# Output projection by seven block products in place of eight: where its weights, its block sums and its order stand in a three-stage encoder kernel

## The chip, the core and the metric

The kernel runs on one NeuronCore of one Trainium2 chip. The core's engines each run their own instruction stream: TensorE (PE in the profile, with its weight loads as PEld), VectorE (DVE), ScalarE (ACT), GpSimd (POOL) and SyncE (SP), which here issues all DMAs. The metric is the device time of one execution in microseconds (us); less is better.

## The reference

One encoder layer over two token streams (a sample of 2048 tokens and a prompt of 1024, both of width 1024). Two branches share one input projection: neighbourhood attention (8 heads of 64) and a gated DeltaNet (4 heads of 128). The last part is what the change touches:

```python
y_a = jnp.einsum('bte,ed->btd', o_a, w_branch_a)
y_b = jnp.einsum('bte,ed->btd', o_b, w_branch_b)
merged = jax.nn.sigmoid(gate_a) * y_a + jax.nn.sigmoid(gate_b) * y_b
return x + jnp.einsum('btd,de->bte', merged, w_out)
```

`o_a` and `o_b` have 512 columns, `merged` and `w_out` have 1024. All data is float32. The kernel writes each float32 operand as a sum of two float16 parts, high and low, scaled by powers of two, and makes each matrix product of three float16 products: high by high, high by low, low by high.

## The kernel before

**Three stages.** The DeltaNet stage makes the hidden activations, the DeltaNet output and the gates, and leaves them in DRAM (`obd`, `szd`, `gtd`). The attention stage loops over four pairs of heads. For each pair it runs 24 projection tiles (`proj_mm`, 24 matmuls `ppn` each) and 24 attention units, one unit and one projection tile per `slot`. A unit runs through several slots: scores (`pS`), softmax, transposes (`pT`), values (`pon`). After the last projection tile the remaining units run in slots of their own; this is called the tail below. The attention output goes to DRAM as `oad`. The output stage takes the tokens in 12 chunks of 256, in the order of the list `order`.

**A chunk of the output stage.** `chunk` loads both branch outputs (`x`), their gate (`y` or `z`) and the sigmoid gates (`th`), multiplies one gate in on POOL (`x<-x,y`), takes the absolute maximum over the chunk (DVE `om<-x`, then a PE transpose `pm` that spreads it over the partitions, then DVE `om<-pm` and three small instructions for a power of two), and splits `x` into high and low parts `op` (ACT high, DVE low). `merged` runs, for each of 8 column tiles `e`, two groups of 12 matmuls of 256 columns (`py_`), one per branch. DVE multiplies each by its gate (`th<-th,py_`), POOL adds the two (`th<-th,th`), ACT and DVE split the sum into `mm`. The output product then runs, for two halves of 128 tokens and two halves of 512 columns, 8 x 3 matmuls of 512 columns (`po_`), and DVE adds each result to the input tile `xo`, which is stored. That is 192 matmuls of 256 columns and 96 of 512 in a chunk.

**What sets the order.** In the DeltaNet and attention stages PE, DVE and ACT are pinned: they keep the order in which the program names the instructions (`TP`, `VP`, `SP` for the attention stage). POOL and SP are ordered by a scheduler. In the output stage before the change all engines are left to the scheduler (`T`, `V`, `S`, `G`, `SY`). Each engine works through its stream in order, so an instruction that waits holds up all behind it. All these calls go through one helper, so the profile shows them all on line 61, and tiles are told apart by name. In the program text the functions stand at: `proj_mm` 1414, `block_out` 1576, `branch_weights` 1597, `early` 1627, `slot` 1653, the tail's loop 1716, `chunk` 1727, `merged` 1754, the output loop 1789.

**Weights.** `w_out` (4 MB) is loaded by 128-column strips and split into `woh` and `wol` at the start of the output stage. In the last pair of the attention stage `branch_weights` loads and splits 16 tiles of `w_branch_a` and `w_branch_b` (ACT `y<-wst,abp`, DVE `y<-wst,abp,y`).

Of the kernel before, what the change touches and what calls it, by code (L numbers as in the profile page):

```python
# [45 lines left out]
def emit(nc, tc, x_prompt, x_sample, norm_g, w_in, attn_q_norm_g, attn_k_norm_g, attn_rpb, dn_conv_w, dn_a_log,  # L46
# [1267 lines left out]
    ps_S = opn("n_S", bufs=NPS[1], space=PSUM)  # L1314
    ps_T = opn("n_T", bufs=NPS[2], space=PSUM)
    ps_O = opn("n_O", bufs=NPS[3], space=PSUM)
    p_mm, ps_mm = pool("n_mm", bufs=NPS[0], side="right", space=PSUM)
    p_Q, ps_Q = pool("n_Q", bufs=1, side="right", space=PSUM)
# [43 lines left out]
    def load_weights(n, src, hi, lo, done, s=None):  # L1362

        def load():
            st = wk.tile([128, src.shape[0] // 128, src.shape[1]], F32, name="wst", tag="xt", bufs=XB)
# [61 lines left out]

    def proj_parts(w, b, t, pp):

        qs = wk.tile([128, 384], F32, name="qs", bufs=QSB)  # L1430
        SP.activation(qs, pp, AF.Copy, scale=2.0 ** -20)
        sq = wk.tile([128, 4, 64], F32, name="sqn", bufs=SQB)
        SP.activation(sq.rearrange("p a b -> p (a b)"), qs[:, 0:256], AF.Square)
        vt = wk.tile([128, 2, 128], F16, name="vt")
# [140 lines left out]

    def block_out(u):

        pO = ps_Q.tile([128, BLK], F32, name="pO", tag="Q") if p_g is None else ps_O.tile([128, BLK], F32, name="pO", tag="o")
        for cb in range(4):
            TP.transpose(pO.rearrange("p (r c) -> p r c", c=64)[:, :, 16 * cb:16 * cb + 16], u.Os[:, cb], ident)  # L1580
        dst = lambda d: d[u.b][128 * u.w.hp:128 * u.w.hp + 128, :]
# [5 lines left out]
            SY.dma_start(dst(oad), ot)  # L1587

        at(0, "dve2", gate)

    def split(src, s, hi, lo, bufs):
        kt = src.shape[0] // 128
        st = wk.tile([128, kt, src.shape[1]], F32, name="wst", tag="xt", bufs=bufs)
        SY.dma_start(st, src.rearrange("(k p) c -> p k c", p=128))
        whl(hi, lo, st, s)

    def branch_weights(n):

# [25 lines left out]
    load_H(4)  # L1624
    load_H(5)

    def early():

        nonlocal ps_g, p_g
        for p in (p_Q, p_mm):  # L1630
            close(p)
        p_g, ps_g = pool("p_g", bufs=3, side="right", space=PSUM)

    ps_g = p_g = None

# [17 lines left out]
    def slot(mm):  # L1653
# [21 lines left out]
        if t:  # L1675
            C.append(t)
        run("dve1")
        for u in E:
            unit_exp(u)
        E.clear()  # L1680
# [8 lines left out]
            B.append((sn + 2, u))  # L1689
        run("act2")  # L1690
        run("dve2")
        work(PW[5], mm)
        sn += 1

    for hp_ in range(4):
        if hp_:
            w = nxt
        if hp_ < 3:
            nxt = pair(hp_ + 1)
            next_pair(nxt)  # L1700
        for b, ats in ((4, ()), (5, (4,)), (0, ()), (1, (0,)), (2, (1,)), (3, (2, 3, 5))):
            if hp_ == 3 and b == 0:
                branch_weights(0)
            for t in range(4):
                mm = proj_mm(w, b, t)
                slot(mm)
                work(1, mm)
# [3 lines left out]
            for a in ats:  # L1711
                for cb in range(4):
                    u = K()
                    u.w, u.b, u.cb = w, a, cb
                    units.append((sn + LA, u))
    while units or B or C or later:
        if p_g is None and done == 48:
            early()
        slot(iter(()))


    order = [8, 9, 0, 1, 2, 3, 4, 5, 6, 7, 10, 11]

    def big(name, *shape):
        return hr.tile([128, *shape], F32 if len(shape) == 3 else F16, name=name, tag="h", bufs=8)

    def chunk(i, pool, **kw):

        c = K()
        c.i, cs = i, slice(TB * (i % 2), TB * (i % 2) + TB)  # L1730
        x = big(f"x{i}", 2, 4, TB)
        y = big(f"y{i}", 2, 4, TB)
        ob, sz = x[:, 1], y[:, 0]
        for t, d in ((x[:, 0], oad), (ob, obd), (sz, szd)):
            SY.dma_start(t, d[i // 2].rearrange("(k p) t -> p k t", p=128)[:, :, cs])
        c.th = [big(f"th{i}{j}", 2, 4, TB) for j in range(2)]
        for j in range(2):
            SY.dma_start(c.th[j].rearrange("p a k t -> p (a k) t"), gtd[i].rearrange("(e j) p t -> j p e t", j=2)[j])
        G.tensor_tensor(ob, ob, sz, op=MUL)
        m = sm.tile([128, 1], F32, name="om")  # L1740
        V.tensor_reduce(m, x.rearrange("p a k t -> p (a k t)"), axis=AX.X, op=MAX, apply_absolute_value=True)
        m2 = sm.tile([128, 1], F32, name="om2")
        allmax(sm, m2, m, (ps_g, "g", 1))
        c.pp, s = sm.tile([128, 1], F32, name="opp"), sm.tile([128, 1], F32, name="osp")
        pow2(m2, c.pp, s, 14)
        op = pool.tile([128, 2, 2, 4, TB], F16, name="op", **kw)
        c.o = [(op[:, j, 0], op[:, j, 1]) for j in range(2)]
        for j in range(2):
            whl(*c.o[j], x[:, j], s)
        m_ = pool.tile([128, 2, 8, TB], F16, name="mm", **kw)  # L1750
        c.mh, c.ml = m_[:, 0], m_[:, 1]
        return c

    def merged(c):

        for e in range(8):
            us = []
            for j in range(2):
                th = c.th[j].rearrange("p a k t -> p (a k) t")[:, e]
                y = ps_g.tile([128, TB], F32, name="py_", tag="g")  # L1760
                gemm(y, wy[e, j][0], wy[e, j][1], c.o[j][0], c.o[j][1], kt=4, t1=TB)
                V.scalar_tensor_tensor(th, in0=th, scalar=1.0, in1=y, op0=ADD, op1=MUL)
                us.append(th)
            G.tensor_tensor(us[0], us[0], us[1], op=ADD)
            S.activation(c.mh[:, e, :], us[0], AF.Copy, scale=2.0 ** -26)
            V.scalar_tensor_tensor(c.ml[:, e, :], in0=us[0], scalar=2.0 ** -26, in1=c.mh[:, e, :], op0=MUL, op1=SUB)

    c0 = chunk(order[0], hr, tag="h", bufs=8)
    merged(c0)
# [6 lines left out]
    ps_o = opn("p_o", bufs=4, space=PSUM)  # L1776

    XB = 4
    woh = pw.tile([128, 8, D], F16, name="woh")
    wol = pw.tile([128, 8, D], F16, name="wol")  # L1780
    for i in range(8):
        cs = slice(128 * i, 128 * i + 128)
        split(w_out[0][:, cs], so_, woh[:, :, cs], wol[:, :, cs], XB)

    fab = pw.tile([128, 1], F32, name="fab")
    V.tensor_tensor(fab, pab, po_, op=MUL)
    V.tensor_scalar_mul(fab, fab, 2.0 ** (-1 + 26 - 42))

    for n, i in enumerate(order):
        c = c1 if n else c0  # L1790
        if n < 11:
            c1 = chunk(order[n + 1], wk)
        if n:
            merged(c)
        xs, ys, t0 = (x_sample[0], y_sample[0], TB * i) if i < 8 else (x_prompt[0], y_prompt[0], TB * (i - 8))
        fo = sm.tile([128, 1], F32, name="ofo")
        V.tensor_tensor(fo, c.pp, fab, op=MUL)
        for t in range(TB // 128):
            ts = slice(128 * t, 128 * t + 128)
            xt = wk.tile([128, D], F32, name="xo", tag="xt", bufs=XB)  # L1800
            SY.dma_start(xt, xs[t0 + 128 * t:t0 + 128 * t + 128, :])
            for n2 in range(2):
                ns = slice(512 * n2, 512 * n2 + 512)
                po = ps_o.tile([128, 512], F32, name="po_", tag="o")
# [5 lines left out]
            SY.dma_start(ys[t0 + 128 * t:t0 + 128 * t + 128, :], xt)  # L1810
    for p in (p_g, p_hr, p_h1, p_nw):
        close(p)
    while stk:
        close(stk.pop())
# [24 lines left out]
```

## Time and profile before

| | |
|---|---|
| median of 3 runs (lowest, highest) | 2895.73 us (2893.43, 2900.97) |
| the profiled execution | 2903.21 us, of which its span 2901.0 us |
| mean granted TensorE clock | 0.978 |
| busy share of the span | PE 94%, PEld 75%, DVE 59%, ACT 47%, POOL 24% |
| DeltaNet stage | to 1718.7 us |
| attention stage | first projection matmul at 1724.8, last at 2310.4; last attention matmul ends at 2393.2 |
| output stage | steady from 2452.6 to the end; first chunk's branch products lie in the attention tail |

The span runs from the first to the last instruction of one execution; all views below are of that execution. A group row names the engine, the operation, the output and input tiles, the shape, the count, and behind the bar the busy time in us and the mean in ns. A timeline row begins with the start and the duration in us and ends with the idle time before it and what ended that. A busy PE is not PE at its peak, since matmuls are pipelined: the spacing of starts says more than durations.

### The profile page before, as it was taken

Reading aid. Unit: us, or ns where it says so; the run is one execution under the profiler, and the core shown is the slowest. Engines: PE = TensorE matmul, PEld = TensorE weight load, DVE = VectorE, ACT = ScalarE, POOL = GpSimd, SP = SyncE. Lnnn points to the kernel's source line nnn. Section 1 sums busy time; section 2 is a strip of 40 time slices with the busy share of each in tenths; the row PEclk is TensorE's granted clock in tenths of the full one; section 3 lists DMA queues with packets and bytes.
Section 4 is the critical chain, followed back from the end, with each engine's and each line's share of the span. In section 5 each row is a group of like instructions: output and inputs, shape, how many; then the busy total and the mean of one; then the engine's idle time right before and its main releaser. Section 6 shows DMA issues by size and latency. Waiting matters only on the chain. (4 is left out here: it accounts for less than half of the span.)

```text
span 2901.0 us, 64328 instructions
## 1 busy us (share of the span) xinstructions
PE 2733.1 (94%) x25046; PEld 2165.8 (75%) x25046; DVE 1714.1 (59%) x4253; ACT 1358.1 (47%) x3777; POOL 704.7 (24%) x1281
## 2 busy tenths in 40 slices
PE   7889999989999999999999989999999888999999
PEld 6777888978788888888789866666666554766765
DVE  7567767577575757747575324576666675443442
ACT  4445455554445545455553434666667652111110
POOL 2232111221111221122210015454444411111211
PEclk9899999999999999999999989999999998999999
DMA  7433442344533543323434357232324458343320
GB/s 255 130 112 87 122 123 83 105 137 120 135 99 95 136 130 105 90 71 100 123 103 120 108 153 186 78 100 79 105 84 122 130 162 257 117 160 131 126 78 30
DMA packets 451743, 347.10 MB, mean 120 GB/s; under 512 B 113012, under 2 KB 414960, under 8 KB 451440
## 3 DMA queue, kind: packets, MB, share of 16 engines
q1 hardware_dynamic: 451439, 343.00, 40.2%
q8 instruction: 197, 3.23, 0.5%
q14 instruction: 107, 0.87, 0.1%
HBM read 252.04 MB, written 90.86 MB: 118 GB/s over the span
## 5 line engine op out<-in xcount | busy, mean ns | idle before, releaser
L61 PE MATMUL pp<-hh,w 128*128 128x256 f16 x6912 | 1210.9, 276 | 25.1 <-DVE thz L61 12.3
L61 PEld LDWEIGHTS <-w 128*128 128x128 f16 x10368 | 1019.8, 99 | 160.8 <-issue 20.1
L61 PE MATMUL pp<-hl,w 128*128 128x256 f16 x3456 | 953.9, 276 | 1.6 <-DMA hl<-hdr 1.2
L61 PE MATMUL ppn<-whi,rh 128*128 128x384 f16 x768 | 252.1, 328 | 6.1 <-DMA rh<-hdr 6.1
L61 PEld LDWEIGHTS <-y 128*128 128x128 f16 x2304 | 226.0, 98 | 41.6 <-issue 13.4
L61 PE MATMUL ppn<-whi,rl 128*128 128x384 f16 x768 | 252.8, 329 | 0.8 <-DMA rl<-hdr 0.8
L61 PE MATMUL ppn<-wlo,rh 128*128 128x384 f16 x768 | 252.0, 328 | 0.0
L61 PEld LDWEIGHTS <-mm 128*128 128x128 f16 x1152 | 112.8, 98 | 133.4 <-issue 0.3
L61 ACT ACTIVATE thz<-pp,wfc 128x256 f32<-128x256 f32 x288 | 123.8, 471 | 175.9 <-PE pp L61 115.4
L61 PEld LDWEIGHTS <-rh 128*128 128x128 f16 x1536 | 145.6, 98 | 77.9 <-issue 8.5
L61 POOL TENSOR_TENSOR th<-th,th 128x256 f32<-128x256 f32 x96 | 69.2, 725 | 402.6 <-DVE th L61 359.7
L61 DVE TENSOR_TENSOR pl<-pT,ph 128x384 f16<-128x384 f32 (+1 forms) x192 | 110.4, 599 | 80.4 <-ACT ph L61 79.2
L61 DVE SCALAR_TENSOR_TENSOR S<-S,egl,pk 128x128 f32<-128x128 f32 x160 | 54.9, 343 | 166.0 <-PE pk L61 139.8
L61 ACT ACTIVATE vn<-pk,nbeg 128x128 f32<-128x128 f32 x176 | 64.8, 368 | 184.6 <-PE pk L61 183.7
L61 ACT ACTIVATE mm<-th 128x256 f16<-128x256 f32 x96 | 40.0, 416 | 225.5 <-POOL th L61 225.5
L61 ACT ACTIVATE Sb<-Sb,nm,pq 128x384 f32<-128x384 f32 (+1 forms) x192 | 140.1, 734 | 1.7 <-DVE nm L61 1.7
L61 DVE CUSTOM_DVE_ANT_0 Sb<-pS,bt 128x384 f32<-128x384 f32 (+1 forms) x192 | 108.4, 597 | 51.9 <-PE pS L61 27.8
L61 POOL TENSOR_TENSOR rqk<-rqk,mhalf 128x4 f32<-128x4 f32 x48 | 51.1, 1064 | 304.0 <-DVE rqk L61 303.8
L61 ACT ACTIVATE Os<-pon,rsn 128x64 f32<-128x64 f32 x192 | 49.7, 310 | 159.7 <-PE pon L61 159.0
L61 PEld LDWEIGHTS <-rl 128*128 128x128 f16 x768 | 75.4, 98 | 61.1 <-issue 29.7
L61 DVE TENSOR_REDUCE wm<-wst 128x1 f32<-128x512 f32 (+1 forms) x111 | 82.2, 761 | 60.9 <-DMA wst<-in_w_in 47.9
L61 ACT ACTIVATE raw<-pp,wfc 128x256 f32<-128x256 f32 x144 | 63.0, 473 | 116.0 <-PE pp L61 111.4
(785 smaller groups left out, 5574.5 us busy)
## 6 DMA issues: line engine op xcount, KB each, us to landing
wst<-in_w_in SPq DMA_DIRECT2D x124, 256.0 KB
gtd<-thz SPq DMA_DIRECT2D x192, 128.0 KB
hh<-hdr SPq DMA_DIRECT2D x48, 512.0 KB
hl<-hdr SPq DMA_DIRECT2D x48, 512.0 KB
th<-gtd SPq DMA_DIRECT2D x24, 1024.0 KB
vw<-vd SPq DMA_DIRECT2D x320, 64.0 KB
IT<-gd SPq DMA_DIRECT2D x48, 256.0 KB
bt<-ud SPq DMA_DIRECT2D x192, 48.0 KB
```

The lines of the kernel that those rows point to most:

```text
L61: i = f(*a, **k)
```

## The change

**Seven products.** The output product is treated as a 2 by 2 block product: `merged` in blocks of 128 tokens by 512 inputs, `w_out` in blocks of 512 by 512. Seven products of sums of blocks (S1 to S4 of `merged`, T1 to T4 of `w_out`, and five single blocks) replace eight products of single blocks. Each is 12 matmuls of 512 columns. The sums of `merged` are made by POOL in `blocks`, four additions or subtractions of 128 x 128 for each of four column pairs `p`, behind one addition of 128 x 512 for the two branches. ACT and DVE split seven blocks in place of four (`split`: pieces of 256, 128 and 512 columns). The products are combined by DVE (`plus`, eight of 128 x 512), one ACT copy and four POOL additions (`add`).

**Weights.** The seven blocks of `w_out` are made in the first three pairs of the attention stage, 16 tiles of 128 rows, by 4 loads, 2 ACT, 2 DVE and 4 POOL instructions and 1 store each (`out_weights`), kept in DRAM as `wod` and loaded as seven tiles `wo` of 1 MB: two in the tail, five after it.

**Order.** The output stage uses the pinned engines, so PE, DVE and ACT run in program order. Chunk 0 and chunk 1 are prepared by named slots at the end of the attention stage (`begin`), chunk 0's branch products are fed into the tail's slots as `filler`, 24 matmuls per slot, and in the output stage chunk n+2 is loaded and prepared while chunk n's product runs and chunk n+1's branch products precede it. The branch products use two PSUM tiles of 512 columns in place of three of 256 columns, and DVE gates both branches by one instruction. `ne` is a new pool for staging tiles.

```diff
+    def merged(c, m):
+        for p in range(4):
+            th = c.th[p // 2][:, 2 * (p % 2):2 * (p % 2) + 2]
+            for e in range(2):
+                y = ps_g.tile([128, 2, TB], F32, name="py_", tag="g")
+                for j in range(2):
+                    ...
+                posts.append((gated, th[:, e], y))
+            posts.append((blocks, c, m, p, th[:, :, 0], th[:, :, 1]))
+    def blocks(c, m, p, u, v):
+        G.tensor_tensor(u, u, v, op=ADD)
+        l, q = (x.rearrange("p a (b t) -> p a b t", b=2) for x in (u, v))
+        G.tensor_tensor(q[:, 0, 0], l[:, 0, 1], l[:, 1, 1], op=ADD)
+        G.tensor_tensor(q[:, 1, 0], l[:, 0, 0], l[:, 0, 1], op=SUB)
+        G.tensor_tensor(q[:, 0, 1], q[:, 0, 0], l[:, 0, 0], op=SUB)
+        G.tensor_tensor(q[:, 1, 1], l[:, 1, 0], q[:, 0, 1], op=SUB)
+        splits.append((c, m, p, l, q))
+    def split(n):
+        for _ in range(n):
+            c, m, p, l, q = splits.pop(0)
+            t = m(p)
+            for d, x in ((slice(0, 2), l[:, :, 0]), (slice(2, 3), l[:, 1:2, 1]), (slice(3, 7), q)):
+                ...
+                parts(x_[:, 0], x_[:, 1], x, 2.0 ** -28)
+        def product(l, r):
+            ps = ps_o.tile([128, 512], F32, name="po_", tag="o")
+            for p in range(4):
+                (mh, ml), (wh, wl) = c.m[p], (wo[r][:, 4 * p:4 * p + 4, h] for h in range(2))
+                TP.matmul(ps, mh[:, l], wh, start=p == 0, stop=False)
+                TP.matmul(ps, mh[:, l], wl, start=False, stop=False)
+                TP.matmul(ps, ml[:, l], wh, start=False, stop=p == 3)
+            return ps
+        SP.activation(u, product(L11, R11), AF.Identity, scale=fo)
+        add(x11, u)
+        yield
+        plus(u, product(S2, T2))
+        add(x12, u)
+        yield
+        plus(u, product(S3, T3))
+        add(x22, u)
+        add(x21, u)
+        yield
+        ps = product(S1, T1)
+        plus(x12, ps)
+        plus(x22, ps)
+        yield
+        plus(x11, product(L12, R21))
+        yield
+        plus(x12, product(S4, R22))
+        SY.dma_start(ys[rows[0], :], xt[0].rearrange("p a b -> p (a b)"))
+        yield
+        plus(x21, product(L22, T4))
+        SY.dma_start(ys[rows[1], :], xt[1].rearrange("p a b -> p (a b)"))
+        yield
+    def run_merged(g):
+        for n, _ in enumerate(g, 1):
+            if n % 24 == 0:
+                old = len(splits)
+                post()
+                if n % 48 == 0:
+                    split(old)
+    run_merged(filler)
+    for n in range(12):
+        ps = iter(())
+        if n < 10:
+            cs_.append(chunk(order[n + 2]))
+            ps = cs_[-1].steps
+            next(ps)
         if n < 11:
-            c1 = chunk(order[n + 1], wk)
-        if n:
-            merged(c)
-        ...
-                for k in range(8):
-                    T.matmul(po, c.mh[:, k, ts], woh[:, k, ns], start=(k == 0), stop=False)
-                    T.matmul(po, c.mh[:, k, ts], wol[:, k, ns], start=False, stop=False)
-                    T.matmul(po, c.ml[:, k, ts], woh[:, k, ns], start=False, stop=(k == 7))
-                V.scalar_tensor_tensor(xt[:, ns], in0=po, scalar=fo, in1=xt[:, ns], op0=MUL, op1=ADD)
+            run_merged(merged(cs_[n + 1], wkm if n % 2 == 0 else nwm))
+        for k, _ in enumerate(output(cs_[n])):
+            post()
+            if k == 1:
+                split(len(splits))
+            if k in (1, 3, 4, 5):
+                next(ps, None)
```

Chunk n+2's steps run at k = 1 (the maximum `om<-x`), k = 3 (the PE transpose `pm`), k = 4 (the power of two and the high parts) and k = 5 (the low parts) of chunk n's output product.

**The order on DVE, in a chunk's output product.** `xo` is the output tile, `po` a product, `u` the running sum of products, `mm` the split parts of the next chunk's merged blocks, `th` the gated branch products, `om` the maximum of the chunk after, `op` its split parts. Before the change:

```order
L61 SCALAR_TENSOR_TENSOR mm<-th_37085,mm 128x256
L61 SCALAR_TENSOR_TENSOR xo<-po__37746,ofo,xo 128x512
L61 SCALAR_TENSOR_TENSOR xo<-po__37772,ofo,xo 128x512
L61 SCALAR_TENSOR_TENSOR xo<-po__37801,ofo,xo 128x512
L61 SCALAR_TENSOR_TENSOR xo<-po__37827,ofo,xo 128x512
L61 TENSOR_REDUCE om_37866<-pm 128x1
```

and now, from the last gated branch product of the next chunk to the spread maximum:

```order
L61 SCALAR_TENSOR_TENSOR th_36865<-th_36865,py__37477 128x512
L61 SCALAR_TENSOR_TENSOR u<-po__37538,ofo,u 128x512
L61 SCALAR_TENSOR_TENSOR mm<-th_36865,mm 128x256
L61 SCALAR_TENSOR_TENSOR mm<-th_36865,mm 128x128
L61 SCALAR_TENSOR_TENSOR mm<-th_36865,mm 128x512
L61 TENSOR_REDUCE om<-x 128x1
L61 SCALAR_TENSOR_TENSOR u<-po__37564,ofo,u 128x512
L61 SCALAR_TENSOR_TENSOR xo<-po__37580,ofo,xo 128x512 x2
L61 SCALAR_TENSOR_TENSOR xo<-po__37597,ofo,xo 128x512
L61 TENSOR_REDUCE om_37561<-pm 128x1
```

The maximum over the chunk after next now stands behind the split of the next chunk's last column pair and behind the second product's sum, all in one output product.

**The order on PE, around the spread of that maximum.** `po` is an output product, `pm` the transpose that spreads the maximum, `py` a branch product with weights `y`. Before the change it stands between the last output product and the next chunk's branch products:

```order
L61 LDWEIGHTS mm
L61 MATMUL po__37827<-woh,mm 128x512
L61 MATMUL pm<-ident,om 128x128
L61 LDWEIGHTS y_31067
L61 MATMUL py__37881<-op,y_31067 128x256
```

and now between the fourth and the fifth of the seven output products:

```order
L61 LDWEIGHTS mm
L61 MATMUL po__38368<-wo_34489,mm 128x512
L61 MATMUL pm<-ident,om 128x128
L61 LDWEIGHTS mm
L61 MATMUL po__38385<-wo_34491,mm 128x512
```

The transpose has moved from the end of the chunk's product to three products before its end.

More of the change, by code (lines that the diff above doesn't have):

```diff
@@ L1576, in block_out @@
     def block_out(u):
[L1578 removed]
+        pO = ps_Q.tile([128, BLK], F32, name="pO", tag="Q")
         for cb in range(4):
@@ new lines, in early, with load_block, out_weights, load @@
+    def early():
+        nonlocal ws, p_ws
+        close(p_ne)
+        p_ws, ws = pool("ws", side="right")
+        for r in (R11, T2):
+            load_block(r, ws)
+    def load_block(r, pool):
+        wo[r] = pool.tile([128, 16, 2, 128], F16, name=f"wo{r}")
+        SY.dma_start(wo[r], wod[r])
+    def out_weights(n, i):
+        p, q = divmod(i, 4)
+        def load():
+            st = ne.tile([128, 4, 128], F32, name="wst", tag="xt", bufs=XB)
+            with tc.issue_after(anchors["last"].ins):
+                for j, (k, c) in enumerate(((0, 1), (0, 0), (1, 0), (1, 1))):
+                    SY.dma_start(st[:, j], w_out[0][256 * p + 128 * k:256 * p + 128 * k + 128, 512 * c + 128 * q:512 * c + 128 * q + 128])
+            at(1, "act", high, st)
+        def high(st):
+            t = ne.tile([128, 7, 2, 128], F16, name="wos", tag="xt", bufs=XB)
+            SP.activation(t[:, 0:3, 0], st[:, 1:4], AF.Identity, scale=so4)
+            at(0, "dve2", low, st, t)
+        def low(st, t):
+            VP.scalar_tensor_tensor(t[:, 0:3, 1], in0=st[:, 1:4], scalar=so4, in1=t[:, 0:3, 0], op0=MUL, op1=SUB)
+            G.tensor_tensor(st[:, 0], st[:, 0], st[:, 1], op=SUB)
+            G.tensor_tensor(st[:, 3], st[:, 3], st[:, 0], op=SUB)
+            G.tensor_tensor(st[:, 2], st[:, 2], st[:, 3], op=SUB)
+            G.tensor_tensor(st[:, 1], st[:, 3], st[:, 1], op=SUB)
+            at(1, "act", sums, st, t)
+        def sums(st, t):
+            SP.activation(t[:, 3:7, 0], st, AF.Identity, scale=so4)
+            at(0, "dve2", rest, st, t)
+        def rest(st, t):
+            VP.scalar_tensor_tensor(t[:, 3:7, 1], in0=st, scalar=so4, in1=t[:, 3:7, 0], op0=MUL, op1=SUB)
+            SY.dma_start(wod[:, :, i].rearrange("r p h c -> p r (h c)"), t.rearrange("p r h c -> p r (h c)"))
+        at(n, "dma", load)
@@ L1638, in emit @@
+    ws = p_ws = None
+    wod = dr.tile([7, 128, 16, 2, 128], F16, name="wod")
+    wo = {}
+    so4 = pcn.tile([128, 1], F32, name="so4")
+    V.tensor_scalar_mul(so4, so_, 0.25)
     units, B, C, E, sn, done = [], [], [], [], 0, 0
@@ L1691, in slot, with begin, load @@
         run("dve2")
+        old = len(splits)
+        post()
+        split(old)
         work(PW[5], mm)
         sn += 1
+    cs_ = []
+    nwm = lambda p: nw.tile([128, 2, 7, 128], F16, name="mm", tag=("whi", "wlo")[p % 2], bufs=2)
+    wkm = lambda p: wk.tile([128, 2, 7, 128], F16, name="mm", bufs=4)
+    def begin(i, ns):
+        cs_.append(chunk(i))
+        def load():
+            with tc.issue_after(anchors["last"].ins):
+                next(cs_[-1].steps)
+        for n, e, f in zip(ns, ("dma", "dve2", "pe", "dve2", "dve2"), (load, *[next] * 4)):
+            at(n, e, f, *() if f is load else (cs_[-1].steps,))
     for hp_ in range(4):
@@ L1700, in emit @@
             next_pair(nxt)
+            for i in range(6 if hp_ < 2 else 4):
+                out_weights(16 + 2 * i, 6 * hp_ + i)
         for b, ats in ((4, ()), (5, (4,)), (0, ()), (1, (0,)), (2, (1,)), (3, (2, 3, 5))):
@@ L1704, in emit @@
             for t in range(4):
+                if hp_ == 3 and b == 3 and t == 2:
+                    begin(order[0], (0, 3, 4, 4, 5))
                 mm = proj_mm(w, b, t)
@@ L1715, in emit @@
                     units.append((sn + LA, u))
+    close(p_mm)
+    p_g, ps_g = pool("p_g", bufs=2, side="right", space=PSUM)
+    filler = iter(())
+    n = 0
+    PW = PT
     while units or B or C or later:
-        if p_g is None and done == 48:
+        if ws is None and done == 48:
             early()
[L1719 to L1766, printed above, removed]
@@ L1768, in emit @@
-    c0 = chunk(order[0], hr, tag="h", bufs=8)
-    merged(c0)
+        n += 1
+        if n == 7:
+            begin(order[1], (0, 3, 4, 4, 5))
+        if n == 6:
+            filler = merged(cs_[0], nwm)
+        slot(filler)
     while stk:
@@ L1811, in emit @@
-    for p in (p_g, p_hr, p_h1, p_nw):
+    ps_o = opn("p_o", bufs=5, space=PSUM)
+    fab = sm.tile([128, 1], F32, name="fab", bufs=1)
+    VP.tensor_tensor(fab, pab, po_, op=MUL)
+    VP.tensor_scalar_mul(fab, fab, 2.0 ** (-1 + 28 + 2 - 42))
+    for r in (T3, T1, R21, R22, T4):
+        load_block(r, pw)
+    def run_merged(g):
+        for n, _ in enumerate(g, 1):
+            if n % 24 == 0:
+                old = len(splits)
+                post()
+                if n % 48 == 0:
+                    split(old)
```

120 lines of the change are left out of this document (82 added, 38 removed).

## The prediction

> **What bounds the kernel now.** I read the page first, then the stretches of the attention and output stages, then the chain of work that ended last and PE's timeline at the border of the two stages, and last the groups for durations. The page:
>
> ```profile
> span 2901.0 us, 64328 instructions
> PE 2733.1 (94%) x25046; PEld 2165.8 (75%) x25046; DVE 1714.1 (59%) x4253; ACT 1358.1 (47%) x3777; POOL 704.7 (24%) x1281
> ```
>
> PE is busy nearly throughout, but the change touches only what lies behind 1725 us, so the stretches matter (span; busy PE, PEld, DVE, ACT, POOL; granted clock; DMA):
>
> ```profile
> 1900.00:2000.00 100.00, 99.41 (x836) 65.79 (x833) 67.78 (x225) 68.13 (x200) 50.24 (x105) 1.00 0.32 91
> 2100.00:2200.00 100.00, 99.08 (x839) 65.75 (x837) 63.55 (x196) 68.37 (x195) 46.87 (x100) 1.00 0.30 83
> 2200.00:2300.00 100.00, 96.88 (x806) 64.00 (x804) 65.24 (x204) 72.81 (x204) 48.15 (x96) 1.00 0.51 146
> 2300.00:2400.00 100.00, 74.58 (x691) 52.94 (x691) 69.19 (x214) 56.57 (x154) 19.36 (x29) 0.90 0.53 158
> 2500.00:2600.00 100.00, 99.16 (x650) 63.60 (x649) 39.77 (x76) 11.04 (x20) 18.57 (x19) 1.00 0.44 146
> ```
>
> PE sets the pace in attention and in output; only the tail (2300 to 2400) leaves PE 25 us idle. In the output stage DVE, ACT and POOL are mostly free. The chain there (start, length, count) is PE alone:
>
> ```profile
> 2452.55 5.18 PE po__34650 L61 x24
> 2495.20 5.18 PE po__35037 L61 x24
> 2532.33 1.31 PE py__35358 L61 x12
> 2537.57 5.18 PE po__35424 L61 x24
> 2875.84 5.18 PE po__38493 L61 x24
> 2891.38 5.19 PE po__38574 L61 x24
> ```
>
> A matmul of 512 columns costs 5.18 / 24 = 0.216 us, one of 256 columns 1.31 / 12 = 0.109. A chunk is 192 x 0.109 = 20.96 us of branch products and 96 x 0.216 = 20.72 of output products, 41.68 in all; its period is 2537.57 - 2495.20 = 42.37 us.
>
> **The products.** 84 matmuls stay of 96: 18.13 us, 2.59 less per chunk, 31.1 over 12 chunks. All of it lies on the path that sets the end, unless something else takes the place. So the question is whether DVE, ACT and POOL, now in a fixed order, follow.
>
> **The new chain beside PE.** The durations, the nearest rows to each new operation:
>
> ```profile
> L61 POOL TENSOR_TENSOR th<-th,th 128x256 f32<-128x256 f32 x96 | 69.2, 725 | 402.6 <-DVE th L61 359.7 <-issue 25.3 <-DVE nm L61 17.6
> L61 POOL TENSOR_TENSOR P<-P,kh 128x512 f32<-128x512 f32 x24 | 30.6, 1275 | 160.8 <-ACT kh L61 160.8
> L61 POOL TENSOR_TENSOR vt<-qs,vt 128x128 f16<-128x128 f32 x96 | 41.0, 427 | 140.7 <-ACT vt L61 140.7
> L61 POOL TENSOR_TENSOR x<-x,y 128x1024 f32<-128x1024 f32 x12 | 28.1, 2345 | 41.5 <-DMA y<-szd 37.7 <-issue 3.8
> L61 DVE SCALAR_TENSOR_TENSOR mm<-th,mm 128x256 f16<-128x256 f32 x96 | 42.5, 443 | 102.8 <-ACT mm L61 102.8
> L61 DVE SCALAR_TENSOR_TENSOR S<-S,egl,pk 128x128 f32<-128x128 f32 x160 | 54.9, 343 | 166.0 <-PE pk L61 139.8
> L61 DVE SCALAR_TENSOR_TENSOR otn<-pO,fo,otn 128x512 f32<-128x512 f32 x24 | 17.9, 746 | 1.0 <-PE pO L61 1.0
> L61 DVE SCALAR_TENSOR_TENSOR y<-wst,abp,y 128x512 f16<-128x512 f32 x16 | 11.5, 745 | 0.0
> L61 DVE TENSOR_REDUCE om<-x 128x1 f32<-128x2048 f32 x12 | 27.4, 2284 | 51.1 <-POOL x L61 51.1
> L61 ACT ACTIVATE mm<-th 128x256 f16<-128x256 f32 x96 | 40.0, 416 | 225.5 <-POOL th L61 225.5
> L61 ACT ACTIVATE y<-wst,abp 128x512 f16<-128x512 f32 x16 | 11.2, 719 | 2.1 <-DMA wst<-in_w_branch_b 1.8 <-DMA wst<-in_w_branch_a 0.3
> ```
>
> No row shows POOL's sum of 128 x 128 in float32. The rows of 256 and 512 columns give 2.1 ns a column, so 0.455 us for 128; the row of 128 with a float16 input has 0.427. I take 0.455; the ends are 0.43 and, if a strided quarter costs what 256 columns do, 0.725.
>
> I count from the start of a chunk's branch products. PE ends a column tile each 2.62 us and a column pair `p` each 5.24. Behind a pair stands a ring that DVE's order closes: gate (0.7), POOL 1.27 + 4 x 0.455 = 3.09, ACT's first high part 0.42, the three split parts of DVE behind ACT 1.65, some 0.05 at each handover: 6.0 us, after which the next pair's gate comes. So the ring is slower than PE. The first pair's gate starts at 5.45, the fourth's ends at 24.2 rather than 21.8. Two PSUM tiles hold: the gates of tiles 3 and 5 end at 12.1 and 18.1, and PE needs them at 13.1 and 18.3.
>
> Then in the output product: the fourth pair's sums end at 27.3, POOL's first addition to `xo` at 28.6, DVE's first sum at 29.3, the three split parts at 30.6, and `om<-x` (2.28) at 32.9. PE's fourth product ends at 20.96 + 4 x 2.59 = 31.3, and the transpose `pm` behind it needs `om`. **So PE waits some 1.65 us for DVE in each chunk**, with three products queued behind it. The rest follows in time: the high parts from 37.2, the first low part at 40.4, and the next branch products start at 40.8. Period: 20.96 + 18.13 + 0.11 + 1.65 = 40.85 us, against 42.37. If the wait is nothing it is 39.2.
>
> POOL's `x<-x,y` of the chunk after next also stands ahead of these sums, and its load of `z` stands on SP behind the store of the upper half (`xo`), whose sum ends at 39.1. From issue to use such a load takes
>
> ```profile
> 2496.49 0.36 SPq L61 DMA_DIRECT2D y<-szd  x1
> 2500.25 2.35 POOL L61 TENSOR_TENSOR x<-x,y 128x1024 f32<-128x1024 f32 x1 [3.78 <-DMA y<-szd]
> ```
>
> 3.76 us, so it lands at 43.3 to 44, the multiplication ends at 46.4, 5.6 us into the next chunk, and the first sums are due at 6.2. It costs nothing; landing 1.5 us later it would cost about 1.
>
> **Steady output stage.** From 2452.55 to 2896.57 (2891.38 + 5.19) stand eleven output products and ten sets of branch products, 444.0 us. Now: nine periods of 40.85, one without `pm` of 39.1, a last product of 18.1: 424.9. Gain 19; 34 without the wait.
>
> **The border.** PE between the stages:
>
> ```profile
> 2392.38 0.83 PE L61 MATMUL pO<-ident,Os 128*128 128x128 f32 x4 [1.22 <-DVE Os L61]
> 2402.39 0.45 PE L61 MATMUL pm<-ident,om 128*128 128x128 f32 x1 [9.18 <-DVE fab L61]
> 2404.49 0.47 PE L61 MATMUL pm<-ident,om 128*128 128x128 f32 x1 [1.66 <-DVE om L61]
> 2406.78 0.37 PE L61 MATMUL py__34398<-op,y 128*128 128x256 f16 x1 [1.82 <-ACT op L61]
> 2408.38 2.50 PE L61 MATMUL py__34398<-op,y 128*128 128x256 f16 x11 [1.22 <-DVE op L61]
> ```
>
> After attention ends at 2393.2, chunk 1 is prepared with PE idle, and PE comes back slow (11 matmuls in 2.50 us). From there to 2452.55, 59.3 us, PE does 41.7 us of products. Now chunk 1 is ready in the tail: 40.85 plus 1 for the weights' loads, gain 17.5. Five loads of 1 MB are issued there; the third product needs its weights 26 us later, so I put little on them. But the tail's DVE takes on chunk 1's preparation (2.28 + 2 x 1.28 + 0.7 = 5.5 us), and splits wait there for POOL: I take 7 us, between 2 and 13. Net gain 10.5.
>
> **The attention stage.** One stall goes:
>
> ```profile
> 2300.01 2.29 DVE L61 TENSOR_REDUCE om<-x 128x1 f32<-128x2048 f32 x1 [4.73 <-POOL x L61]
> 2302.82 0.24 PE L61 MATMUL pon<-vw,pl 128*128 128x64 f16 x1 [4.37 <-DVE pl L61]
> 2303.18 0.51 PE L61 MATMUL ppn<-whi,rh 128*128 128x384 f16 x1
> 2303.49 0.53 PE L61 MATMUL ppn<-wlo,rh 128*128 128x384 f16 x1
> 2307.50 0.33 PE L61 MATMUL ppn<-wlo,rh 128*128 128x384 f16 x1
> ```
>
> Chunk 0's maximum blocked DVE 7 us; PE waited 4.37 and its next matmuls took 0.51 to 0.53 us where the later one took 0.33, some 2 us more. The maximum is now three slots behind its load: gain 6.4, less 1 for POOL's own wait. Against it stand the weights' blocks: per tile DVE 0.6 + 0.75, ACT 0.6 + 0.72, POOL 4 x 0.455, and five DMA issues of some 0.35 us on SP past the units' own loads. That is 43 us of DVE and ACT in 16 tiles. What hides it is PE's own pace; the branch weights are the measure: sixteen tiles of 0.719 + 0.745 in 2160 to 2300, where PE was busy 99.08 and 96.88 in the hundred against 99.41, at most 3 us for 23 us of work. So I take 5, between 0 and 12. Net nothing, between a gain of 5 and a loss of 8.
>
> **Sum.** 19 + 10.5 + 0.5 = 30 us. The profiled execution took 2903.21 (2901.0 and 2.2 around it) and would take 2873; the median is 7.5 us lower than it, and I put the same gain on it: 2895.7 - 30 = **2866 us**.
>
> **The rivals.** (1) *No wait at `pm`.* If ACT and DVE overlap POOL better and the ring keeps to 5.24 us, the 15 us come too: 2851. For it: the wait is a small difference of long chains. Against it: each part has a row. Chance 0.2.
>
> (2) *POOL locks DVE out.* The third split part after DVE's first sum runs while POOL adds to `xo`. The trace has one such meeting:
>
> ```profile
> 2357.74 2.35 POOL L61 TENSOR_TENSOR x<-x,y 128x1024 f32<-128x1024 f32 x1 [0.41 <-DMA y<-szd]
> 2358.74 1.63 DVE L61 SCALAR_TENSOR_TENSOR mm<-th,mm 128x256 f16<-128x256 f32 x1 [0.43 <-ACT mm L61]
> ```
>
> The split took 1.63 for 0.44 and ended 0.3 us behind POOL's. If POOL's addition gets in after the first of the three parts, `om` and with it `pm` come 1.27 us later in each of ten chunks: 13 us, 2879. Chance 0.2. [...]
>
> (3) *POOL's small sums cost what 256 columns do.* At 0.725 each the ring takes 7.1 us, four pairs come 4.3 us later, and PE waits that much more in each of ten chunks: 43 us, 2909, slower than before. It decides from 39 us on, that is 0.70 us for a sum. For it, POOL's cost need not follow the count of columns; four of them, in a power, cost 1.0 us:
>
> ```profile
> L61 POOL TENSOR_TENSOR ssn<-ssn,mhalf 128x4 f32<-128x4 f32 x96 | 96.7, 1008 | 8.0
> ```
>
> Against it: the row of 128 at 0.427. Chance 0.1.
>
> The forecast keeps 0.5.
>
> **How the numbers follow.** About 0.3%, 8.7 us, can be told from no change here. Faster by more is below 2887: nearly all of the forecast (2847 to 2886 with its own bounds), all of the first rival, three quarters of the second: 0.82. Within: the worse ends of the second and of the forecast, part of the third: 0.11. Slower: the rest of the third and a tail in attention: 0.07. The range for 8 in 10 runs from 2841, the first rival with some luck at the border, to 2891, the second with the weights' 12 us; it leaves out the third.
>
> **What would show it.** Right: a period of 40 to 42 us between the first output products of two chunks; an idle time of 1 to 3 us on PE before each `pm` put down to DVE `om`; no idle time over 3 us between the last `pO` and the first `py`; slots of the first pairs as long as before within 0.3 us. Wrong: idle time before `py` put down to DVE `th` in each chunk (the PSUM tiles bind), POOL sums of 128 x 128 over 0.5 us, waits of `po` for `wo` loads, or attention longer by over 15 us.

## The result and the profile after

The changed kernel takes 2926.64 us (median of 4 runs, 2923.97 to 2928.06), the kernel before 2896.06 us (4 runs, 2893.43 to 2900.97). The ratio is 1.0103, 95% interval 1.0085 to 1.0120: 30 us slower where 30 us faster was forecast. The page of the changed kernel:

```profile
span 2924.4 us, 64616 instructions
PE 2728.0 (93%) x24902; PEld 2158.4 (74%) x24902; DVE 1777.2 (61%) x4266; ACT 1393.8 (48%) x3861; POOL 880.7 (30%) x1537
```

PE has 144 matmuls less, as the seven products say. At 0.216 us each they are 31 us, yet PE is busy only 5 us less, and the span grew by 23.4 us. Where, the stretches tell; first those of before (attention until the last projection tile, tail, border, steady output), columns as in the prediction:

```profile
1724.00:2310.50 586.50, 574.75 (x4641) 376.63 (x4642) 357.27 (x1110) 376.76 (x1046) 281.72 (x592) 0.99 0.41 114
2310.50:2393.00 82.50, 66.69 (x651) 48.14 (x649) 60.80 (x194) 51.85 (x141) 12.61 (x18) 0.96 0.53 155
2393.00:2452.50 59.50, 45.63 (x292) 29.74 (x292) 34.76 (x55) 15.94 (x19) 9.75 (x9) 0.83 0.83 261
2452.50:2896.50 444.00, 439.94 (x2986) 292.18 (x2983) 172.38 (x356) 53.42 (x99) 77.11 (x89) 1.00 0.33 111
```

and the same four of the changed kernel:

```profile
1724.00:2334.00 610.00, 585.85 (x4644) 375.91 (x4645) 367.77 (x1145) 392.02 (x1078) 312.94 (x656) 0.99 0.45 130
2334.00:2440.50 106.50, 73.14 (x650) 54.14 (x648) 72.00 (x194) 56.66 (x147) 23.85 (x30) 0.85 0.48 151
2440.50:2481.70 41.20, 40.91 (x277) 27.88 (x276) 21.75 (x37) 7.74 (x15) 17.30 (x24) 0.96 0.50 196
2481.70:2920.00 438.30, 420.66 (x2855) 280.44 (x2853) 225.47 (x352) 76.64 (x149) 203.67 (x253) 0.98 0.37 127
```

The second column is the length of a stretch. Attention is 23.5 us longer, the tail 24.0, the border 18.3 shorter, the steady output stage 5.7 shorter: +23.5. So the loss has three places, not one, and PE idles more in each: 24 us in attention (610.00 less 585.85) against 12, 33 in the tail against 16, 18 in the output stage against 4. The rest of the loss is busy time: in attention and in the tail PE has as many matmuls as before (x4644 for x4641, x650 for x651) and is busy 11.1 and 6.5 us longer. In the tail the granted clock is lower (0.85 for 0.96); in attention it is not, and the profile does not break those 11 us down.

**Output stage.** The wait before `pm` is there, in two sizes:

```profile
2557.08 0.32 PE L61 MATMUL pm<-ident,om 128*128 128x128 f32 x1 [0.28 <-DVE om L61]
2557.24 2.75 PE L61 MATMUL po__35627<-wo,mm 128*128 128x512 f16 x12
2600.14 0.32 PE L61 MATMUL pm<-ident,om 128*128 128x128 f32 x1 [2.13 <-DVE om L61]
2600.30 4.44 PE L61 MATMUL po__36021<-wo,mm 128*128 128x512 f16 x12
```

Six of ten chunks wait 2.13 us, the others 0.3 to 0.7. Behind four of the six the next twelve matmuls take 4.2 to 4.4 us for 2.75. In the branch products ahead of the long wait at 2600 stands this (SP's issue of the gate `z`, POOL's multiplication with it, POOL's sums of the first column pair, and PE):

```profile
2563.79 0.43 SPq L61 DMA_DIRECT2D z<-szd  x1
2571.50 2.35 POOL L61 TENSOR_TENSOR x<-x,z 128x1024 f32<-128x1024 f32 x1 [11.24 <-DMA z<-szd]
2573.81 3.48 POOL L61 TENSOR_TENSOR th<-th 128x512 f32<-128x512 f32 x5
2579.32 2.78 PE L61 MATMUL py__35837<-op,y 128*128 128x256 f16 x24 [1.05 <-DVE th L61]
```

Here `z` is used 7.7 us behind its issue, when the branch products are 6.5 us old; the sums behind it on POOL begin at 2573.8, though DVE had gated the first pair at 2571.1. POOL runs late from then on, through all four pairs. From issue to use it is 6.3 to 7.7 us ahead of all six long waits, and 5.1 to 5.4 ahead of the short ones (the first chunk aside, whose `z` came long before).

**Attention.** A wait of ACT for POOL, at tiles that the kernel before does not have:

```profile
ACT wos L61 <- POOL wst L61: 46.1, 16, 4.1
```

46.1 us in 16 tiles, up to 4.1. One of them, with POOL's last three sums:

```profile
2044.61 1.41 POOL L61 TENSOR_TENSOR wst<-wst 128x128 f32<-128x128 f32 x3
2046.05 0.72 ACT L61 ACTIVATE wos<-wst,so 128x512 f16<-128x512 f32 x1 [2.54 <-POOL wst L61]
2047.70 1.06 ACT L61 ACTIVATE ph<-pT 128x512 f16<-128x512 f32 x2
```

ACT's high parts of the four weight sums stand in program order early in the slot, and POOL, which begins the sums behind DVE's low parts and its own work for the projection, is not done. Behind ACT's wait stand the copy of the projection (`qs`) and the softmax's high part (`ph`) that PE needs.

**Tail.** PE waits 9.7 us in one slot for the loads of the values (`vw`), in four pieces of which the longest is shown; the kernel before waits 5.6 us for them in its tail:

```profile
2354.29 0.43 SPq L61 DMA_DIRECT2D x<-oad  x1
...
2361.73 2.67 SPq L61 DMA_DIRECT2D th<-gtd  x2
...
2366.13 9.89 SPq L61 DMA_DIRECT2D bt<-ud  x13
2376.12 5.12 SPq L61 DMA_DIRECT2D vw<-vd  x8
...
2379.30 0.27 PE L61 MATMUL pon<-vw,ph 128*128 128x128 f16 x1 [7.83 <-DMA vw<-vd]
```

The scheduler has put chunk 1's loads (`x`, `z`, `th`) ahead of thirteen bias loads (`bt`), and those ahead of `vw`.

### The profile page after: what moved, and what is told of

Its sections match the earlier page's. It is cut to its first block, busy times and chain, and to the rows that moved or that the text cites. A ratio compares the mean times of both kernels' runs of the same rounds, so it can differ in the third digit from the quotient of the medians.

```text
span 2924.4 us, 64616 instructions
## 1 busy us (share of the span) xinstructions
PE 2728.0 (93%) x24902; PEld 2158.4 (74%) x24902; DVE 1777.2 (61%) x4266; ACT 1393.8 (48%) x3861; POOL 880.7 (30%) x1537
## 4 chain that ended last, share of the span: by engine, by line
PE 27%; DVE 6%; DMA 6%; POOL 5%; ACT 3%; issue 2%; SPq 1%; POOLq 0%; DVEq 0%; ACTq 0%
PE ppn L61 7%; PE pp L61 6%; POOL th L61 3%; PE pk L61 2%; SPq L61 1%; PE pT L61 1%; PE pon L61 1%; PE pS L61 1%; DVE mm L61 1%; DVE pl L61 1%; DVE om L61 1%; DMA wod<-wos 1%; DMA wst<-in_w_out 1%; DVE th L61 1%; DMA oad<-otn 1%
## 5 line engine op out<-in xcount | busy, mean ns | idle before, releaser
L61 POOL TENSOR_TENSOR th<-th 128x128 f32<-128x128 f32 (+1 forms) x240 | 153.9, 658 | 152.8 <-DVE th L61 145.3
L61 PEld LDWEIGHTS <-mm 128*128 128x128 f16 x1008 | 100.9, 100 | 119.3 <-issue 9.0
L61 ACT ACTIVATE mm<-th 128x256 f16<-128x256 f32 x144 | 59.7, 446 | 245.6 <-POOL th L61 245.6
L61 DVE SCALAR_TENSOR_TENSOR mm<-th,mm 128x256 f16<-128x256 f32 x144 | 86.8, 636 | 61.7 <-ACT mm L61 61.7
```

The costliest lines, as they stand in the source:

```text
L61: i = f(*a, **k)
```

## The experiments

The runs came in three groups, each group with its own runs of the kernel before (medians 2900.14, 2899.34, 2900.59). The ratio to them is the measure; the changed kernel stands at 1.0103, and 0.001 is 2.9 us. Each ratio is known to 3 to 5 us, so a difference from the changed kernel is good to some 6 us; the length of a stage in a trace is the finer measure.

**1. ACT's sums later in the slot.**

```
-            at(1, "act", sums, st, t)
+            at(1, "act2", sums, st, t)
```

> Edit: in the attention stage ACT's high parts of the four weight sums are asked for after the slot's scores, not right behind its first matmuls; nothing else moves. Theory W (the loss in attention is ACT waiting in program order for POOL's sums, 46.1 us in 16 tiles of the changed kernel, with the projection's copies and the softmax queued behind it): ACT's wait for `wst` falls under 10 us, the last projection tile ends near 2318 us, not 2335, and the time falls by 14 to 20 us to about 2909. Rival A (the loss is the amount of work, 43 us of ACT and DVE, and not the wait): the wait falls all the same, but the last projection stays at 2331 or later and the time within 4 us of 2926.6.

Ratio 1.0031 (1.0018 to 1.0044), 2908.46 us: 21 us less. The wait is gone:

```profile
ACT wos L61 <- POOL wst L61: 0.4, 1, 0.4
```

From the first projection matmul to the last it is 594.1 us, not 609.5. Theory W holds for 15 us of the 23; the same work is done, so rival A is out for those. The other 5 to 6 us of the 21 lie within the error of the ratios. In the output stage nothing improved, as its code is the same.

**2. The maximum first.**

```
+            if k in (1, 3, 4, 5):
+                next(ps, None)
             if k == 1:
                 split(len(splits))
-            if k in (1, 3, 4, 5):
-                next(ps, None)
```

> Edit: behind the second of the seven products DVE takes the maximum of the chunk after next ahead of the splits of the next chunk's last column pair, not behind them. Theory M (PE's idle time before `pm`, 0.3 or 2.1 us in each chunk, and its slow matmuls behind the long waits are DVE's order alone): all idle times before `pm` fall under 0.3 us, the mean distance of the first output products of two chunks from 42.0 to about 40.4, and the time by 14 to 18 us to about 2911. Rival B (POOL and DVE work close to the pace of PE, so the wait only moves to the branch products or to the second product): idle times before `py` put down to DVE `th` grow to 1 us or more in most chunks, the distance stays over 41.4 and the time falls by under 7 us.

Ratio 1.0069 (1.0054 to 1.0084), 2920.76 us. No `pm` waits any longer, but PE waits in the branch products, 17.9 us in all:

```profile
2617.51 2.78 PE L61 MATMUL py__36231<-op,y 128*128 128x256 f16 x24 [1.68 <-DVE th L61]
```

In time, 10 us less, it lies between the two expectations; in where the wait went, rival B was right. Ten chunks take 414.9 us, not 420.3. So DVE's order was not the first cause: what is late is what DVE waits for, and there `x<-x,z` again waits for `z` (issued at 2601.34, used at 2609.68).

**3. SP in program order in the tail** (`SY.pin(True)` ahead of its loop, `SY.pin(False)` behind).

> Edit: in the tail SP issues its DMAs in program order in place of the scheduler's. Theory S (the tail's 105 us instead of 82 are for a good part SP's order: the loads `vw` of a unit's values stand behind thirteen bias loads, and PE waits 9.7 us for them): PE's idle time put down to DMA `vw` falls under 2 us, the tail to 95 us or less, the time by 7 to 12 us. Rival D (the tail is long because DVE carries chunk 1's maximum and splits there): the waits for `vw` go but others of the same size, put down to DVE, take their place, and the time stays within 4 us of 2926.6.

Ratio 1.0144 (1.0129 to 1.0159), 2941.86 us: 12 us more, a miss of both. The tail took 121.8 us, with one wait of 13.9 us at `pon`. PE's waits for `vw` add up to 29.4 us, for 9.7. Program order is worse than the scheduler's; the test says nothing on what a better order would give.

**4. No weights' blocks.** The 16 calls of `out_weights` are replaced by seven copies within DRAM, which fill the blocks with other numbers.

> Edit: the blocks of the output weights are not built; seven DMAs within DRAM fill their place with other numbers, so the output is not the reference's. The rest of the program is as in the changed kernel. It bounds what the blocks cost. Theory W and rival A both: the last projection tile ends at 2308 to 2315 us and the time falls by 20 to 26 us. Rival C (the loss is not the blocks but what else moved in attention, the pools and the DMA queue): the last projection stays over 2325.

Ratio 1.0010 (1.0000 to 1.0019), 2902.44 us: 27 us less. Attention takes 586.1 us, that of before is 586.0. So all of its 23.5 us come from the blocks; rival C is out.

**5. The gate's load first.**

```
-            for t, d in ((x[:, 0], oad), (x[:, 1], obd), (z, szd)):
+            for t, d in ((z, szd), (x[:, 1], obd), (x[:, 0], oad)):
```

> Edit: of a chunk's three branch loads the gate `z` is issued first and the attention output last; SP's order then has `z` ahead of the store of the upper half. Theory Z (POOL's multiplication stands ahead of the first column pair's sums and comes late since `z` lands 7.5 to 8.3 us behind its issue, so all later pairs, and with them `pm`, come late in every second chunk): POOL's wait for `z` no longer ends in the branch products, the waits before `pm` are the short ones (0.3 us) in at least eight of ten chunks, the mean distance of the first output products of two chunks falls from 42.0 to 41.0 or less, the time by 8 to 14 us to about 2916. Rival B (POOL and DVE are as slow as PE anyway): the waits stay over 1.5 us in half of the chunks and the time within 4 us of 2926.6.

Ratio 1.0015 (1.0005 to 1.0026), 2904.58 us: 26 us less by one line, about twice what was expected. Two chunks are now 39.69 us apart (2515.36 less 2475.67), all ten alike:

```profile
2475.67 0.32 PE L61 MATMUL pm<-ident,om 128*128 128x128 f32 x1 [0.28 <-DVE om L61]
2515.36 0.32 PE L61 MATMUL pm<-ident,om 128*128 128x128 f32 x1 [0.28 <-DVE om L61]
```

SP's order now has `z` ahead of the store of the upper half (`out_y`), and POOL's multiplication ends before the first sums are due:

```profile
2518.96 0.43 SPq L61 DMA_DIRECT2D z<-szd  x1
2519.43 0.51 SPq L61 DMA_DIRECT2D x<-obd  x1
2521.68 0.35 SPq L61 DMA_DIRECT2D out_y_prompt<-xo  x1
...
2525.79 2.35 POOL L61 TENSOR_TENSOR x<-x,z 128x1024 f32<-128x1024 f32 x1 [7.26 <-DMA x<-obd]
2529.50 3.21 POOL L61 TENSOR_TENSOR th<-th 128x512 f32<-128x512 f32 x5 [1.35 <-DVE th L61]
```

`x<-obd`, now the last of the two, still takes 6.4 us from its issue to its use; it is only issued earlier. In the 14 us from 2560 of the changed kernel the DMA engines were close to full:

```profile
2560.00:2574.00 14.00, 14.00 (x107) 10.31 (x106) 7.27 (x12) 2.19 (x2) 2.76 (x3) 1.00 0.93 325
```

0.93 busy, 325 GB/s: `z` stood behind `xo`, two loads of `x` and a store. Theory Z holds: long waits before `pm` need a late `z`. Its size was put too low (41.0 us or less a chunk, and 39.69 came).

**6. Both.** Edits 2 and 5 together.

> Edit: both the gate's load first and the maximum ahead of the last pair's splits. Theory Z with M: no wait before `pm` nor before `py` over 0.5 us, distance of two chunks 39.3 to 39.9 us (20.96 + 18.13 and some 0.4 at the borders), the time falls by 20 to 25 us to about 2904. Rival B: distance over 40.8, the idle times come back before `py`, the time falls by less than 14 us.

Ratio 0.9995 (0.9985 to 1.0005), 2897.28 us, 31 us less than the changed kernel where 20 to 25 were expected. Two chunks are 39.20 us apart, without any wait, as the forecast has it "if the wait is nothing". With `z` in time DVE's order is worth another 0.49 us a chunk. It also parts two instructions that had met: DVE's three splits of the last column pair and POOL's `xo<-xo,u`. First run 5, where they stand side by side, then run 6, where the maximum runs beside POOL instead:

```profile
2510.82 2.29 DVE L61 SCALAR_TENSOR_TENSOR mm<-th,mm 128x256 f16<-128x256 f32 x3
2510.98 1.37 POOL L61 TENSOR_TENSOR xo<-xo,u 128x512 f32<-128x512 f32 x1 [0.86 <-DVE u L61]
```

```profile
2513.05 1.27 POOL L61 TENSOR_TENSOR xo<-xo,u 128x512 f32<-128x512 f32 x1 [0.86 <-DVE u L61]
2515.08 1.22 DVE L61 SCALAR_TENSOR_TENSOR mm<-th,mm 128x256 f16<-128x256 f32 x3
```

The splits take 2.29 us beside POOL, in the chunks of the changed kernel as in those of run 5, and 1.22 without it: 1.07 us, of which 0.49 at most reach PE here.

**7. Chunk 1 later in the tail**: `if n == 11:` for `if n == 7:`.

> Edit: chunk 1's preparation begins in the tail's eleventh slot, not its seventh; SP's order then has five bias loads (`bt`) ahead of chunk 1's loads, not behind them. Theory S (what stands on SP ahead of the bias and value loads costs PE its 9.7 us for `vw`): PE's idle time for `vw` falls to 4 us or less and the tail from 107 to 100 us or less, the time by 5 to 9 us. Rival P (the tail is long since PE keeps to its written order, 24 branch products in each slot, and stands still behind a waiting `pon` while such products are left; before, the scheduler had placed them in the gaps): the wait goes to another place, the tail stays over 104 us.

Ratio 1.0057 (1.0039 to 1.0076), 2917.52 us: 13 us less. The tail takes 93.9 us. SP's order there:

```profile
2348.73 1.36 SPq L61 DMA_DIRECT2D bt<-ud  x3
...
2353.32 0.82 SPq L61 DMA_DIRECT2D bt<-ud  x2
2354.19 0.42 SPq L61 DMA_DIRECT2D x<-oad  x1
...
2362.92 5.04 SPq L61 DMA_DIRECT2D bt<-ud  x8
2368.07 4.37 SPq L61 DMA_DIRECT2D vw<-vd  x7
```

Five bias loads are out of the way before chunk 1's loads, and PE's wait for `vw` falls from 9.7 us to under 2. That is theory S, and more than it asked for. The edit also moves chunk 1's maximum and splits on DVE by four slots.

**8. Chunk 1 prepared behind the tail.**

> Edit: chunk 1 is loaded and prepared behind the tail. Theory D (chunk 1's maximum and splits on DVE and its loads are what lengthens the tail): the tail falls from 107 to 96 us or less, and PE stands idle some 12 to 18 us between the tail and chunk 1's branch products, so the time rises by 2 to 10 us. Rival P (PE's written order): the tail stays over 101 us and the time rises by 9 to 16 us.

Ratio 1.0077 (1.0062 to 1.0092), 2922.37 us. The tail takes 93.8 us, as theory D had it, but so it did in run 7, with chunk 1's work left in. So the place of that work costs the 13 us, not its amount on DVE. That it is the place in SP's order is shown for the wait for `vw`; the place in DVE's order moved with it and was not tested by itself. PE idled only 6.5 us behind the tail, where 12 to 18 were expected.

**9. The four together** (edits 1, 2, 5 and 7).

> Edits: the four that helped, together: the gate's load first, the maximum ahead of the splits, chunk 1 from the tail's eleventh slot, ACT's sums behind the scores. Theory (the changed kernel lost to four waits in different stages, and the seven products themselves bring what was counted): the gains add, 29 us in output, 18 in attention, 9 to 13 in the tail, so 2866 to 2871 us; distance of two chunks 39.2. Rival (a wait taken out in one stage comes back in the next, since the stages share SP and POOL): 2880 us or more.

Ratio 0.9893 (0.9878 to 0.9908), 2871.20 us against 2900.59: 29 us faster than before, 61 less than the changed kernel. The single gains are 21, 31 (runs 2 and 5 as run 6) and 13, together 65: they add but for 4 us. 2871.20 us is 0.2 above the upper end of what was expected. Its tail and its steady output stage:

```profile
2322.00:2415.00 93.00, 68.34 (x653) 51.40 (x652) 72.54 (x196) 56.53 (x147) 22.40 (x32) 0.88 0.58 174
...
2456.00:2866.00 410.00, 409.51 (x2849) 278.85 (x2846) 215.89 (x353) 75.94 (x149) 198.12 (x253) 1.00 0.39 134
```

In the output stage PE is busy 409.51 of 410.00 us at a clock of 1.00, and no wait is left there.

**10. Eight products in the new order.** Edits 2, 5 and 7; `blocks` only adds the branches, four weight blocks without sums, and in `output`:

```
+        for t, (x, l1, r1, l2, r2) in enumerate(((x11, L11, R11, L12, R21), ...
+            product(ps, l1, r1, True, False)
+            yield
+            product(ps, l2, r2, False, True)
+            plus(x, ps)
```

> Edit: the new order of the program, with the gate's load first, the maximum ahead of the splits and chunk 1 from the eleventh slot, but with eight products of single blocks: no sums of blocks on POOL, four weight blocks in place of seven. It tells what the seventh product less is worth by itself. Theory (the products' 2.59 us in a chunk are real and all on the path): distance of two chunks 41.8 to 42.0 us against 39.2; last projection tile near 2316 as without the wait for POOL; 2888 to 2900 us, some 25 us above the four edits together. Rival (the order alone makes the gain): within 10 us of the four edits together.

Ratio 0.9967 (0.9953 to 0.9981), 2892.35 us, 21 us above run 9. Two chunks are 41.79 us apart,

```profile
2480.84 0.27 PE L61 MATMUL pm<-ident,om 128*128 128x128 f32 x1
2522.63 0.27 PE L61 MATMUL pm<-ident,om 128*128 128x128 f32 x1
```

against 39.20: 2.59 us, to the hundredth the twelve matmuls. Over twelve chunks that is 31 us. What the sums of blocks cost elsewhere is 593.5 (run 9) less 589.0 in attention and 92.9 less 88.0 in the tail: 9 us. So the products' 31 us less these 9 make the 21, and the theory holds: the order alone doesn't make the gain. (The seven products use six single blocks, three of each side, and DVE adds them in seven instructions, not the five and eight named above.) The order alone (run 10 against before, in the medians) is worth 8 us.

**11. The weights' sums on DVE**, as run 9, but with `VP` for `G` in the four sums and edit 1 undone.

> Edits: as the four together, but the weights' sums are made by DVE in place of POOL, and ACT's high parts stand where the change put them. Theory W (the wait for POOL is the loss in attention, not where ACT's work stands): ACT waits under 10 us in all for the sums, the last projection tile ends at 2314 to 2320 us as with ACT later, the time within 5 us of the four together. Rival A (the amount of work on the engines in order counts): the last projection is at 2325 us or later, the time 8 us or more above the four together.

Ratio 0.9917 (0.9900 to 0.9933), 2878.52 us, 7 us above run 9. ACT still waits 15.5 us for the sums, now DVE's, and 13.4 us for DVE's low parts in `wos` (8.6 in run 9); attention takes 598.4 us. Theory W's bounds (10 us of wait, 5 us of time) are missed, and so are rival A's (2325 us for the end of the projection, 8 us of time): it lies between the two. Moving the work to an engine in order does less than moving the reader.

**12. The filler one slot earlier** (`if n == 5:`), on run 9.

> Edits: the four together, and chunk 0's branch products begin one slot earlier in the tail, in the fifth. Theory P (what is left of the tail's length is PE in written order, idle behind waits with branch products still to do): the earlier slots have idle time to take them, the tail is 1 to 4 us shorter. Rival D (each slot is as long as its chain on DVE and ACT whatever PE does): the tail stays within 1 us.

Ratio 0.9901 (0.9883 to 0.9919), the same as run 9 within the intervals. The tail of its trace is 100.7 us, not 92.9: chunk 0's low parts aren't ready and PE waits for them,

```profile
2342.08 0.58 PE L61 MATMUL py__33426<-op,y 128*128 128x256 f16 x2 [5.52 <-DVE op L61]
```

It tells neither theory from the other.

## Why the prediction was wrong

The forecast has the trace 30 us shorter, and it came 23.5 longer. Of these 53.5 us 24 lie in attention (18.5 of cost above the 5 forecast, and a gain of 5.4 that did not come), 17 in the tail, and 13.4 in the output stage (438.3 for 424.9); the border is 0.8 better. Of the signs of being wrong that were named, "attention longer by over 15 us" showed.

**The products: right.** 2.59 us in each chunk, all on the path (run 10).

**The border: right.** 17.5 forecast, 18.3 measured.

**"So the ring is slower than PE": wrong.** The ring was put at 6.0 us by adding POOL's five sums, ACT's first part and all three split parts of DVE. With `z` in time POOL's sums follow each other at PE's pace:

```profile
2534.78 3.22 POOL L61 TENSOR_TENSOR th<-th 128x512 f32<-128x512 f32 x5 [2.07 <-DVE th L61]
2536.07 0.62 ACT L61 ACTIVATE mm<-th 128x256 f16<-128x256 f32 x2 [2.70 <-POOL th L61]
2537.19 0.95 DVE L61 SCALAR_TENSOR_TENSOR mm<-th,mm 128x256 f16<-128x256 f32 x2
...
2540.06 3.22 POOL L61 TENSOR_TENSOR th<-th 128x512 f32<-128x512 f32 x5 [2.06 <-DVE th L61]
```

2540.06 less 2534.78 is 5.28 us. ACT's first parts begin 1.29 us into POOL's 3.22, since they need only the first of the five sums, and two of DVE's three parts lie beside the others. A path was added up as if it had no branches. In the undisturbed chunk the wait at `pm` is 0.28 us, not 1.65. That the ten waits of the changed kernel have a mean of 1.44 us, near the forecast, is luck: they are long or short by when `z` comes, not by the ring.

**"It costs nothing; landing 1.5 us later it would cost about 1": the first half was wrong.** The mechanism and its place were named. But the row for issue to use (3.76 us) was of a load ahead of which SP had issued none for 16 us; here it stood behind two loads of `x`, one of `xo` and a store, and took 5.1 to 7.7. `z` in time is worth 2.34 us a chunk (42.03, the mean of ten distances, less 39.69), 23 us in all. Without this loss the stage would have come out at 415, ten less than the 424.9 forecast, as the ring had been put too slow.

**"What hides it is PE's own pace; the branch weights are the measure": wrong**, 23.5 us for 5. A branch weight tile goes DMA, ACT, DVE. A block tile goes DMA, ACT, DVE, POOL, ACT, DVE, and the second ACT stands in an order written by hand, ahead of POOL's end. Of the 23.5 us 15.4 are this wait (609.5 less 594.1, run 1), 3.0 the single blocks (589.0 in run 10 less 586.0), for which the measure was right, and the 5.1 left are put down to the sums' own work and buffers, by difference. The bound of 12 was too narrow because every hiding place was looked for on PE, and none on ACT, behind whose wait PE's input is queued.

**"One stall goes": it stayed.** The maximum no longer blocks DVE, but the bias loads do, as SP issues chunk 0's five loads ahead of them: DVE's second score sum waits 10 us, and PE behind it 4.12:

```profile
2329.40 0.69 DVE L61 CUSTOM_DVE_ANT_0 Sb<-pS,bt 128x512 f32<-128x512 f32 x1 [10.02 <-DMA vd<-vt]
2330.15 0.58 PE L61 MATMUL pS<-kh,qh 64*128 64x512 f16 x1 [4.12 <-DVE mx L61]
```

The profile names the DMA that SP issued right behind the last bias load; that it is the bias which the sum waits for is a reading of the order, not tested.

**The tail: 7 forecast (2 to 13), 24 measured.** The forecast counted DVE's added work. 13 us came from the place of chunk 1's preparation (runs 7 and 8), some 8 of them as the wait for `vw` behind SP's order, and 5 from the sums and seven-block splits (run 10 against run 9). The last 5.5 us (88.0 less 82.5) are open. In run 10's tail PE waits 5.3 us for DVE at `Os`, 3.0 at `om` and 2.9 at `kl`, where the kernel before waits 1.2 at `Os`. PE in a written order where a scheduler had filled gaps may be the reason, but run 12 did not test it, as it ran into another wait.

**The rivals.** No wait at `pm` (2851) is what the output stage became once `z` was on time (0.28 us left) and the maximum stood first (none). The meeting of DVE's splits with POOL's addition, the second rival, came in every chunk: the three splits took 2.29 us beside it and 1.22 without (runs 5 and 6), 1.07 more, near the 1.27 forecast. But as the ring is quicker than forecast, 0.49 us of it at most reached PE with `z` in time. How much of the long waits of 2.13 us it is was not measured. POOL's small sums cost nearly what was assumed:

```profile
L61 POOL TENSOR_TENSOR th<-th 128x128 f32<-128x128 f32 x128 | 61.1, 499 | 5.0
```

0.50 us each, far from the 0.70 at which the third rival decides. The forecast gave 0.07 to a slower kernel, as its three rivals all lay in the output stage; the two largest losses lay in attention and its tail, which the change seems only to pass through.

## What to carry to other kernels

Where an engine keeps to a written order, look at each new instruction on it for the producer it waits for and for what is queued behind it; 43 us of hidden work cost 8, and one reader placed too early in its slot cost 15. A load's time from issue to use was 3.76 us where SP had issued none ahead of it for 16 us, and 5.1 to 7.7 behind two loads of `x`, one of `xo` and a store: take it from a row with the same loads ahead of it, and put the load that an in-order engine multiplies with ahead of those that have time. Order transfers by who stops without them, not by the sequence in which the code names the tiles.

## What the runs showed of the hardware

Behind four of six idle times of 2.13 us PE's clock fell. The granted clock (the third column from the end) in the 4 us behind the long wait at 2600 and behind the short one at 2557:

```profile
2557.00:2561.00 4.00, 3.92 (x19) 1.91 (x20) 3.04 (x6) 0.00 (x0) 2.50 (x2) 1.00 0.00 0
2600.00:2604.00 4.00, 3.86 (x12) 1.60 (x13) 2.16 (x4) 0.00 (x0) 2.49 (x2) 0.63 0.01 4
```

0.63 against 1.00, and the wait of 2.13 us costs 1.69 more (4.44 less 2.75). Of the six waits of this length four were followed by slow matmuls, with a clock of 0.57 to 0.66 in the 4 us behind them; behind the other two and behind the short ones it stayed at 1.00, and ahead of each it was 1.00. What parts the four from the two these runs do not show.
